# One decoder layer in split float32 on one core: where the low half of a sum is taken, where x is added, and how the first weights lie in memory

## The chip, the cores and the metric

The program runs on 1 core of one Trainium2 chip (trn2). The metric is device microseconds of one execution; the figure of a kernel is the median of its timed runs.

## The reference

A layer with two token mixers, 256 tokens of width 2048. Cut to what matters here:

```
h = rms_norm(x, norm_g)
proj = h @ w_in                                   # 2048 x 11264
q, k, v, z_a, u_b, v_b, z_b, g_a, g_b = split(proj)
att = moba_attention(rms_norm(q), rms_norm(k), v) # 8 heads, causal inside one block of 256
y_a = (att * silu(z_a)) @ w_proj_a
sgu = spatial_gating(gelu(u_b), gelu(v_b), sgu_norm_g, w_s, b_s)
y_b = (sgu * silu(z_b)) @ w_proj_b
merged = sigmoid(g_a) * y_a + sigmoid(g_b) * y_b
return x + merged @ w_out
```

All data are float32, and nearly all of the work is in the products with w_in, w_proj_a, w_proj_b and w_out.

## The kernel before, in words

**Splitting.** Each float32 operand is held as a high half (a cast to the type fp32r) and a low half (the value less its high half). A product is three matmuls of 128x512: low by high, high by high, high by low (`three`, line 415 and after; all of them have line 422 in the profile).

**Granules.** The weights come as 120 granules of 128x2048 float32 (1 MB), in the order of `schedule`. The blocks "quad" (q, k, v, za, vb, ub, zb, four g, two out, 8 granules each) multiply a 2x2 grid of blocks. A granule whose number is in the first tuple of its row in `SETS` is done by a Strassen-like form in seven products, 21 matmuls (`seven`); the others are done directly in eight, 24 matmuls (`direct`). The second tuple of the row is the order in which the granules of the block come. Between the g blocks stand the "proj" granules, 24 matmuls each. In the text below a granule of seven products is called S, one of eight D.

**The work on a granule ahead of its matmuls** is in `split`. For D: ACT casts the words to `wh` (line 244), DVE takes the low half in place (line 245). For S three sums of 512 columns are needed as well: `t[0]` (line 274), `t[1:3]` (line 275, which reads `t[0]`), their high half `th` by ACT (line 277), the low half of the words, 2048 columns in one instruction (line 279), and then the low half of the sums, 1536 columns (line 280). Before `t[0]` one block has to be added to another: in q, k and v DVE does that (line 272), in the later blocks a DMA adds in memory, from a copy of the block in a ring of 12 buffers (`pre_copy`, `pre_sum`), and the sum is loaded in place of the block.

**Order.** Every engine runs its list in the order in which the code emits it. Granule i's loop emits the loads of granule i+5 on SP, the matmuls of i on PE, and then the splits up to granule i plus its number in `LEADS`. All else (norms, softmax, transposes, evacuations) hangs on the loop by tables: `HOOKS` gives for each step its block, granule and place (pre, mid, late, evac, post), `EVAC` does so for the evacuation of PSUM and `SECOND` for the second half of a transposition. The words lie in six buffers (`words0` to `words5`, granule number modulo 6); a buffer takes its next load when PE is done with it. SP issues nearly all loads, strictly in order: an issue that has to wait holds back every later one.

**The start.** `LOADS` sets the order of the first loads: the first quarters of granule 0, the first columns of x, and so on. Granules 0 to 3 are loaded in pieces (`cuts`: four, four, two and two). While the first data come, 11 matmuls on zeros run (`ps_w`, line 322).

**The end.** The two out blocks (granules 104 to 111 and 112 to 119) each make four results of 128x512. `early` combines the S products of a block in SBUF tiles `e[0..3]`, and `residual` (lines 715 to 721) then adds x: in block 1 by DVE, from x in SBUF; in block 0 POOL issues four DMAs that add x to `e[j]` in SBUF (line 718), and SP stores each `e[j]` to the output (line 719). `post_out` later adds the D products of block 0 to the stored output, again by DMAs from POOL that add in memory (line 728).

Of the kernel before, what the change touches and what calls it, by code (L numbers as in the profile page):

```python
# [19 lines left out]
ALU = mybir.AluOpType  # L20
# [23 lines left out]
SETS = {("q", 0): ((), (0, 1, 2, 3, 4, 5, 6, 7)), ("k", 0): ((0, 1, 2, 3, 4), (5, 1, 3, 4, 6, 0, 2, 7)),  # L44
# [8 lines left out]
        ("out", 0): ((0, 1, 2, 4), (3, 2, 0, 6, 1, 7, 4, 5)),  # L53
        ("out", 1): ((0, 1, 2, 3, 4), (0, 5, 1, 2, 3, 4, 7, 6))}
SCRATCH = ("za", "vb", "ub", "zb", "g", "out")
LEADS = {("q", 0): (3, 2, 2, 3, 3, 3, 3, 2), ("k", 0): (2, 3, 3, 2, 3, 3, 3, 2),
# [16 lines left out]
SECOND = {("turn_m", 0): (1, "mid"), ("turn_m", 2): (1, "post"), ("turn_z", "za"): (1, "mid"),
          ("turn_qk", "q"): (1, "late"), ("mix", 0): (1, "mid"), ("turn_z", "zb"): (0, "post"),
          ("turn_qk", "k"): (1, "mid"), ("turn_m", 1): (1, "pre")}
HOOKS = [
    ("q", 0, 0, "pre", "split_x", 2), ("q", 0, 0, "pre", "split_x", 3), ("k", 0, 1, "evac", "root", "q", 2),
    ("q", 0, 1, "evac", "split_x", 5), ("q", 0, 2, "post", "split_x", 6), ("q", 0, 3, "mid", "split_x", 7),
    ("v", 0, 3, "late", "squares", "k", 3), ("q", 0, 4, "pre", "keep_vec"),
    ("ub", 0, 2, "pre", "squares", "vb", 0), ("ub", 0, 2, "evac", "squares", "vb", 1),  # L80
    ("q", 0, 5, "post", "forms", "x", "x"), ("vb", 0, 0, "mid", "func", "za", AF.Silu),
# [9 lines left out]
    ("v", 0, 3, "late", "norm", "k", 1), ("v", 0, 2, "late", "squares", "k", 2),
    ("k", 0, 4, "evac", "root", "q", 3), ("v", 0, 5, "late", "norm", "k", 2),
    ("v", 0, 0, "mid", "squares", "k", 0), ("q", 0, 1, "mid", "split_x", 4), ("zb", 0, 3, "late", "spatial"),
    ("proj", 3, 0, "evac", "func", ("g", 3), AF.Sigmoid), ("ub", 0, 3, "late", "root", "vb", 0),
# [50 lines left out]
def hybrid_layer_kernel(  # L145
# [54 lines left out]
    def f(ap):  # L200
        return ap.bitcast(F32)
# [729 lines left out]
```

## Time and profile before

| what | us |
|---|---|
| three timed runs | 661.92, 664.0, 933.4 |
| median | 664.0 |
| the profiled execution, its own time | 663.75 |
| its span, first to last instruction | 662.0 |
| PE busy / DVE busy / ACT busy in the span | 650.6 / 609.5 / 438.6 |

The span lies 1.75 us below the time of its own execution. A row of the timeline gives the start, the duration, the engine and line, the operation with what it writes and reads, the shape, and in brackets the idle time of the engine before it with what ended it. A row of the waits gives who waited for whom: the total, the number of times and the longest. In the names of the profile `words3float` is buffer 3 as it was loaded and `words3float32r` the same bytes as low halves. Matmuls overlap, so the cost of one is read from the distance of two starts and not from the duration.

### The profile page before, as it was taken

The page shows a single profiled execution, that of the slowest core. Times are in us where ns is not written, and L with a number is a line of the kernel's source. Part 1 is how long each engine was busy: PE and PEld are TensorE (multiplying, and loading weights), DVE is VectorE, ACT ScalarE, POOL GpSimd, SP SyncE. Part 2 cuts the span into 40 slices and gives each one's busy share as a digit, 9 for nine tenths or more (in the row PEclk, how much of TensorE's full clock was granted, in tenths as well). Part 3 has the DMA queues.
Part 4 walks back from the last instruction along what each step waited for, and adds up shares of the span by engine and source line. Part 5 has one row for each costly group of instructions (what it writes and reads, how often), then busy time and mean ns, then how long its engine had stood idle before and what let it go on. Part 6 is the DMA issues. An engine that isn't in the chain of part 4 may idle for free.

```text
span 662.0 us, 8169 instructions
## 1 busy us (share of the span) xinstructions
PE 650.6 (98%) x2956; PEld 535.5 (81%) x2956; DVE 609.5 (92%) x532; ACT 438.6 (66%) x547; POOL 89.7 (14%) x91
## 2 busy tenths in 40 slices
PE   9999999999999999999999999999999999999977
PEld 5888788888888888888887888888888888888855
DVE  4799999999999999999999999899978998999955
ACT  7969796968787598687556736655653567456540
POOL 1001323400010206210010011010101001100300
PEclk9999999999999999999999999999999999999979
DMA  8995587797777987986698579869966987974981
GB/s 298 417 364 204 203 253 254 228 260 220 230 211 247 271 258 235 282 255 238 189 324 252 171 228 338 266 218 313 288 227 209 328 264 233 259 237 169 165 278 63
DMA packets 46407, 164.71 MB, mean 249 GB/s; under 512 B 5152, under 2 KB 5792, under 8 KB 37792
## 3 DMA queue, kind: packets, MB, share of 16 engines
q1 hardware_dynamic: 36432, 146.11, 61.2%
q0 software_dynamic: 9360, 17.04, 16.6%
q10 hardware_dynamic: 576, 1.05, 0.4%
q8 instruction: 23, 0.38, 0.2%
q14 instruction: 16, 0.13, 0.1%
HBM read 159.46 MB, written 29.88 MB: 286 GB/s over the span
## 4 chain that ended last, share of the span: by engine, by line
PE 46%; DVE 36%; DMA 7%; issue 6%; ACT 3%; SPq 1%; POOL 0%; DVEq 0%; ACTq 0%; POOLq 0%
PE y L422 13%; PE acc_g L422 12%; PE seven_g L422 8%; PE acc_out L422 3%; PE acc_vb L422 2%; DVE sums0float32r L280 2%; PE acc_za L422 2%; DVE words2float32r L279 2%; DVE sums1float L275 2%; DVE sums2float32r L280 2%; PE seven_za L422 2%; DVE sums1float32r L280 2%; DVE sums0float L275 2%; DMA words5float<-in_w 2%; DMA cut_float<-in_w 2%
## 5 line engine op out<-in xcount | busy, mean ns | idle before, releaser
L229 POOL DMA_DIRECT2D ring<-in_w x51 | 43.4, 862 | 296.2 <-DMA ring<-in_w 288.6
L277 ACT CAST th<-sums1float 128x1536 fp32r<-128x1536 f32 x21 | 31.2, 1484 | 43.2 <-DVE sums1float L275 41.3
L277 ACT CAST th<-sums2float 128x1536 fp32r<-128x1536 f32 x20 | 29.7, 1486 | 45.1 <-DVE sums2float L275 45.1
L277 ACT CAST th<-sums0float 128x1536 fp32r<-128x1536 f32 x20 | 29.7, 1484 | 41.5 <-DVE sums0float L275 41.5
L367 POOL TENSOR_TENSOR rs<-ms,mhalf 128x4 f32<-128x4 f32 x12 | 30.4, 2533 | 74.9 <-DVE ms L366 74.9
L422 PE MATMUL acc_g<-wh,xuh 128*128 128x512 f32 x99 | 38.6, 389 | 0.0
L422 PE MATMUL acc_g<-wh,xul 128*128 128x512 f32 x99 | 38.6, 389 | 0.0
L280 DVE TENSOR_TENSOR sums1float32r<-sums1float,th 128x1536 fp32r<-128x1536 f32 x21 | 36.8, 1753 | 1.4 <-ACT th L277 1.4
L280 DVE TENSOR_TENSOR sums2float32r<-sums2float,th 128x1536 fp32r<-128x1536 f32 x20 | 35.1, 1753 | 0.0
L280 DVE TENSOR_TENSOR sums0float32r<-sums0float,th 128x1536 fp32r<-128x1536 f32 x20 | 35.1, 1753 | 0.0
L279 DVE TENSOR_TENSOR words2float32r<-words2float,wh 128x2048 fp32r<-128x2048 f32 x13 | 29.8, 2292 | 1.3
L245 DVE TENSOR_TENSOR words1float32r<-words1float,wh 128x2048 fp32r<-128x2048 f32 x10 | 22.9, 2288 | 7.1 <-ACT wh L244 7.1
L245 DVE TENSOR_TENSOR words5float32r<-words5float,wh 128x2048 fp32r<-128x2048 f32 x12 | 27.4, 2286 | 1.9 <-ACT wh L244 1.9
L422 PE MATMUL acc_out<-wh,ml 128*128 128x512 f32 x65 | 25.7, 396 | 2.2 <-ACT wh L267 2.2
L279 DVE TENSOR_TENSOR words4float32r<-words4float,wh 128x2048 fp32r<-128x2048 f32 x11 | 25.2, 2291 | 0.8
L422 PE MATMUL acc_out<-wh,mh 128*128 128x512 f32 x65 | 25.6, 393 | 0.0
L422 PE MATMUL y<-wh,zal 128*128 128x512 f32 x64 | 25.2, 394 | 0.0
L422 PE MATMUL acc_q<-wh,xuh 128*128 128x512 f32 x64 | 25.2, 393 | 0.0
L422 PE MATMUL y<-wh,zbl 128*128 128x512 f32 x64 | 25.0, 391 | 0.0
L422 PE MATMUL acc_q<-wh,xul 128*128 128x512 f32 x64 | 25.0, 391 | 0.0
L422 PE MATMUL y<-wh,zah 128*128 128x512 f32 x64 | 25.0, 390 | 0.0
L422 PE MATMUL y<-wh,zbh 128*128 128x512 f32 x64 | 24.9, 390 | 0.0
(992 smaller groups left out, 2172.8 us busy)
## 6 DMA issues: line engine op xcount, KB each, us to landing
words5float<-in_w SPq DMA_DIRECT2D x14, 1024.0 KB, 7.8
ring<-in_w SPq DMA_DIRECT2D x51, 256.0 KB, 7.4
ring<-in_w POOLq DMA_DIRECT2D x51, 256.0 KB, 7.2
words1float<-in_w SPq DMA_DIRECT2D x12, 1024.0 KB, 6.5
words4float<-in_w SPq DMA_DIRECT2D x11, 1024.0 KB, 8.9
words3float<-in_w SPq DMA_DIRECT2D x11, 1024.0 KB, 7.0
words0float<-in_w SPq DMA_DIRECT2D x9, 1024.0 KB, 7.1
words2float<-in_w SPq DMA_DIRECT2D x11, 768.0 KB, 6.9
```

The source lines that it names most:

```text
L229: nc.gpsimd.dma_start(pre[i], w[i, :, 2 * B:3 * B], accum_op=ALU.add)
L245: nc.vector.tensor_tensor(l, r, f(h), op=ALU.subtract)
L275: nc.vector.tensor_tensor(*(ap.rearrange("p (a n) -> p a n", n=B) for ap in (t[:, B:], r[:, 2 * B:])), t[:, None, 0:B].to_broadcast([P, 2, ...
L277: nc.scalar.copy(th[i], t)
L279: nc.vector.tensor_tensor(wl[i], r, f(wh[i]), op=ALU.subtract)
L280: nc.vector.tensor_tensor(tl[i], t, f(th[i]), op=ALU.subtract)
L367: nc.gpsimd.tensor_tensor(dst, ms[:, :n], mhalf[:, :n], op=ALU.pow)
L422: nc.tensor.matmul(acc, a, b, start=(start and n == 0), stop=(stop and n == 2))
```

## The change

**1. Sums.** The low half of the sums of an S granule (before: line 280, right behind the words' low half) is kept back and emitted by `settle`: between the two sums of the next granule if that is S, ahead of its split if it is D.

**2. Half tiles.** The words of an S granule are two tiles of 128x1024, loaded by separate DMAs, cast by two ACT instructions and turned to low halves by two DVE instructions.

**3. x.** In out block 0 SP stores `e[j]` first, and POOL's DMA then adds x to the stored output in memory. `post_out` adds the rest as before.

**4. Layout.** The host lays each piece of granules 0 to 3 (`CUTS`) in one run of memory; the piece had been rows of 2 or 4 KB at steps of 8 KB.

**5. Tables.** k does four granules by sevens in place of five (7 x 3 = 21 matmuls become 24 for one granule). The other blocks keep their number of S granules; orders, leads, hooks and evacuation places are new. The matmuls on zeros are 8 in place of 11, and one pair of the `four_forms` subtractions is swapped.

The diff, with the tables cut to `SETS` and the hooks at the start of the program:

```diff
-SETS = {("q", 0): ((), (0, 1, 2, 3, 4, 5, 6, 7)), ("k", 0): ((0, 1, 2, 3, 4), (5, 1, 3, 4, 6, 0, 2, 7)),
+SETS = {("q", 0): ((), (0, 1, 2, 3, 4, 5, 6, 7)), ("k", 0): ((0, 1, 2, 3), (5, 3, 4, 1, 6, 0, 2, 7)),
...
-        ("out", 0): ((0, 1, 2, 4), (3, 2, 0, 6, 1, 7, 4, 5)),
-        ("out", 1): ((0, 1, 2, 3, 4), (0, 5, 1, 2, 3, 4, 7, 6))}
+        ("out", 0): ((0, 1, 2, 4), (3, 0, 5, 6, 1, 2, 4, 7)),
+        ("out", 1): ((0, 1, 2, 3, 4), (5, 2, 3, 0, 4, 1, 6, 7))}
...
-    ("q", 0, 0, "pre", "split_x", 2), ("q", 0, 0, "pre", "split_x", 3), ("k", 0, 1, "evac", "root", "q", 2),
-    ("q", 0, 1, "evac", "split_x", 5), ("q", 0, 2, "post", "split_x", 6), ("q", 0, 3, "mid", "split_x", 7),
...
+    ("q", 0, 0, "post", "split_x", 5), ("q", 0, 2, "late", "split_x", 7), ("v", 0, 3, "mid", "squares", "k", 3),
...
+CUTS = {0: 4, 1: 4, 2: 2, 3: 2}
...
+    HW = WORDS // 2
+    halfs = [[both(f"half{n}_{j}_", HW, base + 8 * KB * n + j * 4 * KB) for j in range(2)] for n in range(RAWS)]
...
     def load_piece(i, a, b):
-        nc.sync.dma_start(raw[i][:, a:b], w[i, :, a:b])
+        src = w[i, :, a:b]
+        if i in CUTS:
+            n = WORDS // CUTS[i]
+            j = a // n
+            src = bass.AP(tensor=w.tensor, offset=w.offset + (i * WORDS + j * n) * P + a - j * n,
+                          ap=[[n, P], [1, b - a]])
+        nc.sync.dma_start(raw[i][:, a:b], src)
...
             nc.sync.dma_start(raw[i][:, 0:B], pre[i])
-            load_piece(i, B, WORDS)
+            load_piece(i, B, HW)
+            load_piece(i, HW, WORDS)
             return
+        if strassen(i):
+            pieces = 2
...
         if i in pre:
-            nc.scalar.copy(wh[i], r)
+            nc.scalar.copy(wh[i][:, 0:HW], h0)
+            nc.scalar.copy(wh[i][:, HW:], h1)
             mid()
...
-        nc.vector.tensor_tensor(t[:, 0:B], r[:, 0:B], r[:, B:2 * B], op=ALU.subtract)
-        nc.vector.tensor_tensor(*(ap.rearrange("p (a n) -> p a n", n=B) for ap in (t[:, B:], r[:, 2 * B:])),
+        nc.vector.tensor_tensor(t[:, 0:B], h0[:, 0:B], h0[:, B:HW], op=ALU.subtract)
+        settle()
+        nc.vector.tensor_tensor(*(ap.rearrange("p (a n) -> p a n", n=B) for ap in (t[:, B:], h1)),
                                 t[:, None, 0:B].to_broadcast([P, 2, B]), op=ALU.subtract)
         nc.scalar.copy(th[i], t)
         late()
-        nc.vector.tensor_tensor(wl[i], r, f(wh[i]), op=ALU.subtract)
-        nc.vector.tensor_tensor(tl[i], t, f(th[i]), op=ALU.subtract)
+        nc.vector.tensor_tensor(l0, h0, f(wh[i][:, 0:HW]), op=ALU.subtract)
+        nc.vector.tensor_tensor(l1, h1, f(wh[i][:, HW:]), op=ALU.subtract)
+        unsettled.append((i, t))
+
+    unsettled = []
+
+    def settle(i=NG):
+        if unsettled and unsettled[0][0] <= i:
+            n, t = unsettled.pop()
+            nc.vector.tensor_tensor(tl[n], t, f(th[n]), op=ALU.subtract)
...
-    for _ in range(11):
+    for _ in range(8):
         nc.tensor.matmul(ps_w, warm[:, 0:P], warm, start=True, stop=True)
...
             if c == 0:
-                nc.gpsimd.dma_start(e[j], part(x, c, j), accum_op=ALU.add)
                 nc.sync.dma_start(part(out, c, j), e[j])
+                nc.gpsimd.dma_start(part(out, c, j), part(x, c, j), accum_op=ALU.add)
...
         plain = i < 8
+        settle(i)
...
+    for i, n in CUTS.items():
+        g[i] = g[i].reshape(P, n, WORDS // n).transpose(1, 0, 2).reshape(P, WORDS)
```

**SP at the end, before.** The issues from the last load of granule 116 (`words2`) to the loads of granule 117 (`words3`) and 118; in brackets what each waits for (DMASW are DMAs that POOL issued, DMAHW those of the other queues).

```order
L217 DMA words2float_59<-in_w 128x1536 [waits DMAHW7_49]
L719 DMA out<-out_c_4605 128x512 [waits DMAHW0_49,DMASW1_49]
L719 DMA out<-out_c_4608 128x512 [waits DMAHW1_49,DMASW2_49]
L719 DMA out<-out_c_4607 128x512 [waits DMAHW2_49,DMASW3_49]
L719 DMA out<-out_h 128x512 [waits DMAHW3_49,DMASW4_49]
L236 DMA words3float_61<-ring_121 128x512 [waits DMASW0_49,DMAHW4_49,DVE_49,PE_49]
L217 DMA words3float_61<-in_w 128x1536 [waits DMAHW5_49]
L217 DMA words4float_63<-in_w 128x2048 [waits DMAHW6_49,DVE_49,PE_49]
```

The same place in the changed kernel (`half_0_79` and `half_1_81` are buffer 3).

```order
L226 DMA half_1_float_77<-in_w 128x1024 [waits DMAHW2_49]
L746 DMA out<-out_c_4792 128x512 [waits DMAHW3_49,Activation_49]
L746 DMA out<-out_c_4795 128x512 [waits DMAHW4_49,DVE_49]
L746 DMA out<-out_c_4794 128x512 [waits DMAHW5_49,DVE_49]
L746 DMA out<-out_h 128x512 [waits DMAHW6_49,DVE_49]
L247 DMA half_0_float_79<-ring_145 128x512 [waits DMAHW7_49,DMASW0_49,PE_49]
L226 DMA half_0_float_79<-in_w 128x512 [waits DMAHW0_49]
L226 DMA half_1_float_81<-in_w 128x1024 [waits DMAHW1_49]
L226 DMA words4float_63<-in_w 128x2048 [waits DMAHW2_49,PE_49]
```

The four stores stand at the same place, ahead of granule 117's loads; they wait for the engines that make `e[j]` and no longer for POOL's DMAs.

**DVE in a run of S granules, before** (three granules in out block 1; `sums` are the sums of a granule, `th` their high half).

```order
L274 TENSOR_TENSOR sums1float_93<-words0float_55 128x512
L275 TENSOR_TENSOR sums1float_93<-words0float_55,sums1float_93 128x1024
L279 TENSOR_TENSOR words0float32r<-words0float_55,wh_4664 128x2048
L280 TENSOR_TENSOR sums1float32r<-sums1float_93,th_4665 128x1536
L274 TENSOR_TENSOR sums2float_95<-words1float_57 128x512
L275 TENSOR_TENSOR sums2float_95<-words1float_57,sums2float_95 128x1024
L279 TENSOR_TENSOR words1float32r<-words1float_57,wh_4698 128x2048
L280 TENSOR_TENSOR sums2float32r<-sums2float_95,th_4699 128x1536
```

The same engine in a run of S granules of out block 1 in the changed kernel.

```order
L293 TENSOR_TENSOR sums0float_115<-half_0_float_67 128x512
L308 TENSOR_TENSOR sums2float32r<-sums2float_119,th_4757 128x1536
L295 TENSOR_TENSOR sums0float_115<-half_1_float_69,sums0float_115 128x1024
L299 TENSOR_TENSOR half_0_float32r<-half_0_float_67,wh_4852 128x1024
L300 TENSOR_TENSOR half_1_float32r<-half_1_float_69,wh_4852 128x1024
L293 TENSOR_TENSOR sums1float_117<-half_0_float_71 128x512
L308 TENSOR_TENSOR sums0float32r<-sums0float_115,th_4853 128x1536
L295 TENSOR_TENSOR sums1float_117<-half_1_float_73,sums1float_117 128x1024
L299 TENSOR_TENSOR half_0_float32r<-half_0_float_71,wh_4862 128x1024
L300 TENSOR_TENSOR half_1_float32r<-half_1_float_73,wh_4862 128x1024
```

The instruction of line 280 (now 308) has moved from the end of its own granule to between the two sums of the next, and the words' low half is two instructions of half the width.

More of the change, by code (lines that the diff above doesn't have):

```diff
@@ L73 @@
[L73 to L74 removed]
+SETS = {("q", 0): ((), (0, 1, 2, 3, 4, 5, 6, 7)), ("k", 0): ((0, 1, 2, 3), (5, 3, 4, 1, 6, 0, 2, 7)),
[8 rows of a table added]
+        ("out", 0): ((0, 1, 2, 4), (3, 0, 5, 6, 1, 2, 4, 7)),
+        ("out", 1): ((0, 1, 2, 3, 4), (5, 2, 3, 0, 4, 1, 6, 7))}
+SCRATCH = ("za", "vb", "ub", "zb", "g", "out")
+LEADS = {("q", 0): (3, 2, 2, 2, 2, 3, 3, 2), ("k", 0): (2, 3, 3, 2, 2, 2, 2, 2),
[5 rows of a table added]
+         ("out", 1): (3, 2, 3, 3, 3, 3, 3, 2), ("proj", 0): (3, 2, 3, 3), ("proj", 1): (2, 2, 3, 3),
+         ("proj", 2): (2, 2, 3, 2), ("proj", 3): (3, 3, 3, 2)}
@@ new lines @@
+EVAC = {("proj", 0): (0, "late"), ("proj", 1): (0, "evac"), ("proj", 2): (1, "mid"), ("proj", 3): (0, "late"),
+        ("g", 2, "quad"): (0, "late"), ("zb", 0, "early"): (1, "late"), ("out", 1, "quad"): (0, "evac"),
+        ("g", 3, "quad"): (0, "mid"), ("k", 0, "early"): (0, "evac"), ("vb", 0, "quad"): (1, "pre"),
+        ("v", 0, "quad"): (0, "mid"), ("g", 0, "early"): (0, "late"), ("g", 1, "early"): (0, "evac"),
+        ("v", 0, "early"): (0, "pre"), ("out", 1, "early"): (1, "late"), ("out", 0, "quad"): (0, "evac"),
+        ("za", 0, "early"): (0, "pre"), ("g", 3, "early"): (0, "evac"), ("q", 0, "quad"): (0, "mid"),
+        ("out", 0, "early"): (1, "mid"), ("zb", 0, "quad"): (1, "pre"), ("ub", 0, "early"): (0, "evac"),
+        ("vb", 0, "early"): (0, "evac"), ("za", 0, "quad"): (0, "evac"), ("ub", 0, "quad"): (1, "late"),
+        ("g", 2, "early"): (1, "pre"), ("q", 0, "early"): (1, "late"), ("k", 0, "quad"): (0, "evac"),
+        ("g", 0, "quad"): (0, "mid")}
@@ L91 @@
[L91 to L94, printed above, removed]
-    ("g", 0, 0, "mid", "func", "zb", AF.Silu), ("ub", 0, 3, "evac", "squares", "vb", 2),
-    ("ub", 0, 6, "evac", "norm", "vb", 1), ("v", 0, 4, "late", "root", "k", 2),
@@ new lines @@
+    ("q", 0, 2, "evac", "split_x", 6), ("za", 0, 2, "late", "soft_max", 0), ("zb", 0, 0, "post", "mix", "E"),
[5 rows of a table added]
+    ("ub", 0, 5, "evac", "norm", "vb", 1), ("proj", 3, 0, "mid", "turn_m", 2, (0, 1), "L01"),
+    ("zb", 0, 3, "evac", "spatial"), ("ub", 0, 3, "late", "squares", "vb", 3), ("q", 0, 3, "mid", "load_nat"),
[3 rows of a table added]
+    ("proj", 2, 0, "late", "func", ("g", 2), AF.Sigmoid), ("za", 0, 1, "post", "score", "E"),
+    ("ub", 0, 7, "pre", "norm", "vb", 3), ("za", 0, 4, "mid", "soft_exp", 1),
+    ("proj", 0, 1, "post", "func", ("g", 0), AF.Sigmoid), ("vb", 0, 0, "late", "turn_p", 0, "E012"),
@@ new lines @@
+    ("ub", 0, 4, "evac", "norm", "vb", 0), ("q", 0, 6, "pre", "stats"), ("za", 0, 3, "late", "soft_max", 1),
+    ("v", 0, 5, "post", "norm", "k", 3), ("ub", 0, 6, "evac", "norm", "vb", 2), ("q", 0, 2, "mid", "split_x", 4),
+    ("proj", 3, 2, "mid", "halves_h", "m"), ("vb", 0, 2, "post", "attend", 1, "E23"),
+    ("v", 0, 0, "post", "root", "k", 0), ("q", 0, 0, "pre", "split_x", 2), ("za", 0, 5, "post", "soft_sum", 1),
+    ("ub", 0, 3, "evac", "root", "vb", 0), ("proj", 3, 1, "post", "forms", "mf", "m"),
@@ new lines @@
+    ("k", 0, 4, "late", "norm", "q", 0), ("k", 0, 1, "mid", "squares", "q", 1),
+    ("v", 0, 4, "late", "root", "k", 2), ("ub", 0, 1, "post", "func", "vb", AF.Gelu_apprx_tanh),
+    ("k", 0, 7, "late", "norm", "q", 3), ("proj", 3, 2, "post", "halves_l", "m"),
+    ("proj", 3, 2, "post", "turn_m", 1, (0, 1), "L23"), ("ub", 0, 2, "late", "squares", "vb", 1),
+    ("out", 0, 0, "in", "turn_m", 3, (0, 1), "E01"), ("out", 0, 2, "late", "forms_m4"),
+    ("out", 0, 3, "mid", "halves_m4"), ("g", 0, 5, "post", "gate_b"), ("vb", 0, 1, "in", "turn_p", 1, "E301"),
@@ L117 @@
+    ("proj", 1, 0, "mid", "func", ("g", 1), AF.Sigmoid), ("vb", 0, 2, "late", "load_mix"),
+    ("proj", 3, 1, "post", "func", ("g", 3), AF.Sigmoid), ("q", 0, 5, "late", "forms_5"),
     ("out", 1, 2, "post", "load_res", 1),
```

65 lines of the change are left out of this document (21 added, 44 removed), and 40 rows, old and new, of tables (HOOKS, LEADS, SETS).

## The prediction, made before the changed kernel ran

> **What bounds the kernel now.** First the page, for who is busy; then the chain of waits, for the rate at which PE runs when nothing holds it; then what PE waited for; then the timeline at those places.
>
> ```profile
> span 662.0 us, 8169 instructions
> PE 650.6 (98%) x2956; PEld 535.5 (81%) x2956; DVE 609.5 (92%) x532; ACT 438.6 (66%) x547; POOL 89.7 (14%) x91
> ```
>
> ```profile
> 422.22 21.79 PE y L422 x96
> ```
>
> PE is busy for 98% of the span, DVE for 92%. In the chain 96 matmuls of 128x512 take 21.79 us, 0.227 us each; that is PE's own pace, and only time beyond it can be won without taking matmuls away. DVE is second in line and close. Where PE stood still:
>
> ```profile
> PE acc_out L422 <- ACT wh L267: 2.2, 1, 2.2
> PE acc_out L422 <- DVE words3float32r L279: 1.4, 1, 1.4
> ...
> PE acc_g L422 <- DVE words2float32r L279: 0.9, 1, 0.9
> PE acc_k L422 <- DVE words2float32r L279: 0.5, 1, 0.5
> ```
>
> Two waits at the end of the program and two on DVE at granules with sums are all that reach half a microsecond once the layer's matmuls have begun; each costs more than its row says.
>
> **The stall at the end.**
>
> ```profile
> 635.07 0.39 PE L422 MATMUL acc_out<-sums0float32r,mh 128*128 128x512 f32 x1
> 637.68 0.69 PE L422 MATMUL acc_out<-wh,ml 128*128 128x512 f32 x1 [2.22 <-ACT wh L267]
> ...
> 641.17 0.63 PE L422 MATMUL acc_out<-wh,F5h 128*128 128x512 f32 x1
> 641.60 0.63 PE L422 MATMUL acc_out<-words3float32r,F5h 128*128 128x512 f32 x1
> ...
> 644.84 0.39 PE L422 MATMUL seven_out<-th,F5h 128*128 128x512 f32 x1
> ```
>
> and, as a row of the stages (busy time of PE, PEld, DVE, ACT and POOL, then granted clock, DMA share and GB/s):
>
> ```profile
> 634.80:645.00 10.20, 6.63 (x17) 4.45 (x17) 8.17 (x5) 7.13 (x5) 0.00 (x0) 0.67 0.70 259
> ```
>
> From 635.07 to 644.84 lie 14 starts. At 0.227 they take 3.2 us; they took 9.8. The stall costs 6.6 us, of which the two waits are 3.6. The rest is the pace afterwards: starts 0.43 us apart, with a granted clock of 0.67 in that window.
>
> Why it stood:
>
> ```profile
> 611.02 0.59 ACT L727 COPY late<-acc_out 128x512 f32<-128x512 f32 x1 [0.77 <-PE acc_out L422]
> 615.05 0.88 POOL L718 DMA_DIRECT2D out_h<-in_x  x1 [0.29 <-issue]
> 614.76 6.21 SPq L719 DMA_DIRECT2D out<-out_c  x3
> 622.92 0.33 SPq L719 DMA_DIRECT2D out<-out_h  x1
> 623.42 1.91 SPq L236 DMA_DIRECT2D words3float<-ring  x1
> 635.75 0.69 DVE L274 TENSOR_TENSOR sums1float<-words3float 128x512 f32<-128x512 f32 x1 [5.62 <-DMA words3float<-in_w]
> ```
>
> PE was done with the last granule of out block 0 by 611.02, so buffer 3 was free. But SP stood in front of its four stores, each of which waited for POOL's addition of x to land, until 622.92. Only then did it issue granule 117's load (623.42), which took until 635.7: 12.3 us.
>
> **The change, part by part.**
>
> *x in memory.* The stores now wait for DVE's and ACT's four tiles alone. In the rows, POOL's last addition, which needed the last of these tiles, was issued at 615.05, so all tiles were there by then. Four stores at the 0.33 us of the single issue are 1.3 us: granule 117's load goes out at about 616.4 (615.05 + 1.3) instead of 623.42. With the same 12.3 us it lands at 628.7. DVE had its previous sums done at 635.75 - 5.62 = 630.1. So the load is 1.4 us early and the stall goes: **-6.6**. What is late next: the additions to the output. They are as many as before:
>
> ```profile
> out<-out_c SPq DMA_DIRECT2D x6, 256.0 KB, 2.7
> out<-late POOLq DMA_DIRECT2D x4, 256.0 KB, 9.0
> ```
>
> Store, addition of x, addition of the rest: 2.7 + 9.0 + 9.0 us plus eight issues on POOL of 0.88 (7 us) from 616 end near 644, ahead of the end at about 653. On POOL nothing but these additions is queued there. Cost 0; without that cover it is the last rival below.
>
> *Sums and half tiles.* One granule on DVE, start to start:
>
> ```profile
> 332.96 0.69 DVE L274 TENSOR_TENSOR sums2float<-words0float 128x512 f32<-128x512 f32 x1
> 333.68 1.23 DVE L275 TENSOR_TENSOR sums2float<-words0float,sums2float 128x1024 f32<-128x1024 f32 x1
> 335.00 2.29 DVE L279 TENSOR_TENSOR words0float32r<-words0float,wh 128x2048 fp32r<-128x2048 f32 x1
> 337.21 1.75 DVE L280 TENSOR_TENSOR sums2float32r<-sums2float,th 128x1536 fp32r<-128x1536 f32 x1
> 338.88 0.68 DVE L274 TENSOR_TENSOR sums0float<-words1float 128x512 f32<-128x512 f32 x1
> 137.08 1.88 DVE L484 TENSOR_TENSOR v_c<-acc_v,v_c 128x512 f32<-128x512 f32 x3
> 16.84 4.63 DVE L245 TENSOR_TENSOR cut_float32r<-cut_float,wh 128x1024 fp32r<-128x1024 f32 x4 [0.26 <-ACT wh L244]
> ```
>
> The period is 5.92: 0.72 + 1.32 + 2.21 + 1.67. Three instructions of 512 columns that do not wait for each other take 1.88, 0.60 from start to start; four of 1024 take 4.63, 1.14 each. So the second sum, which reads the first, costs 0.12 extra, and what follows it 0.18. With the late low half between the two sums the first gap goes; if the half tile frees the second gap as well, the period is 0.60 + 1.67 + 3 x 1.14 = 5.69, a gain of 0.23. If it does not, 5.87, a gain of 0.05; if each half pays the gap instead, 6.05 to 6.2, a loss of up to 0.3. I take 0.1 to 0.2: the independent rows are the nearer ones, since the first half touches nothing that the second sum reads or writes. Over the 34 such granules up to the first g block (5 + 5 + 5 + 4 + 4 + 6 + 5) that is 3 to 7 us of DVE. In k there is more:
>
> ```profile
> 77.20 0.68 DVE L272 TENSOR_TENSOR words2float<-words2float 128x512 f32<-128x512 f32 x1
> 83.93 2.28 DVE L245 TENSOR_TENSOR words3float32r<-words3float,wh 128x2048 fp32r<-128x2048 f32 x1
> ```
>
> A granule by sevens costs 6.73 there, a direct one 2.2: 4.5 us of DVE less, for three matmuls more, 3 x 0.227: **+0.7**. ACT does two casts for one; it idles for a third of the span.
>
> What PE gets of this is only its stalls. The largest:
>
> ```profile
> 347.93 0.39 PE L422 MATMUL acc_g<-wh,xuh 128*128 128x512 f32 x1
> 349.20 0.50 PE L422 MATMUL acc_g<-words2float32r,xuh 128*128 128x512 f32 x1 [0.89 <-DVE words2float32r L279]
> ```
>
> 1.27 between starts, 1.04 lost, for a wait shown as 0.9. The two rows of waits on DVE sum to 1.4; scaled alike, with smaller ones and some after-effect, 2 to 2.8. DVE's relief exceeds each of them, so I take **-2.3** (bounds 0, if the new tables put other work in front, and -2.8).
>
> *Layout, warm matmuls and the first hooks.*
>
> ```profile
> 1.25 4.88 PE L322 MATMUL ps_w<-warm 128*128 128x512 bf16 x11 [1.25 <-DVE warm L319]
> 5.47 0.62 ACT L244 CAST wh<-cut_float 128x512 fp32r<-128x512 f32 x1 [1.44 <-DMA cut_float<-in_w]
> 7.20 0.39 PE L422 MATMUL acc_q<-wh,xuh 128*128 128x512 f32 x1
> 13.13 0.40 PE L422 MATMUL acc_q<-wh,xuh 128*128 128x512 f32 x1
> 13.74 0.50 PE L422 MATMUL acc_q<-cut_float32r,xuh 128*128 128x512 f32 x1 [0.21 <-DVE cut_float32r L245]
> ```
>
> The first matmul needs ACT's first cast, which waits for a landing until 5.47 and ends at 6.09; it does not follow the warm run. Pieces in one run can only land earlier or alike; nothing in the trace prices it: 0 to -1, and I take **-0.5**, about the loss before 13.74 (0.61 less 0.227) and a little of the first landing. The warm run shrinks to 8/11 of 4.88, 3.5 us, and ends near 4.8, over 1 us before the data. I take 0 for that and price it below.
>
> Sum on the span: 662.0 - 6.6 + 0.7 - 2.3 - 0.5 = 653.3. Around the span lie 663.75 - 662.0 = 1.75 us: **655.1**. The median of the runs, 664.0, is within 0.3 of the profiled one.
>
> **The rivals.**
>
> *A cold start.* After the stall at the end, starts were 0.43 apart from 637.68 to 644.6, 7 us, though PE had work. If the gap after the shorter warm run does the same, 7 us from 6.1 on hold 16 matmuls that each lose 0.2: 3.2, less the 0.5 booked above. 657.8. For it: before, PE came to full pace at about 7.2, right after an unbroken run from 1.25. Against it: the gap would be some 1.3 us, half of the 2.6 between the starts at 635.07 and 637.68.
>
> [...]
>
> *The stall stays.* The load's margin is 1.4 us, and it now shares the DMA engines with the additions in memory. A landing 4 us later brings the stall and the slow pace back: 655.1 + 6.6 = 661.7. For it: the 12.3 us of the late load. Against it: DVE may be further ahead, and PE needs granule 117 only at 635.
>
> *DVE gains nothing for PE*, or the new orders bring as many stalls: 655.1 + 2.3 + about 1 = 658.4. For it: the low half of the sums did not wait for ACT before either.
>
> *Slower: the additions become the end.* All eight write one output. If each waits for the one before to land, 8 x 9.0 = 72 us from 616 end at 688, some 690 us. It decides once the chain passes about 652, that is 36 us or four landings. Against it: before, the four additions of line 728 were issued apart by less than a landing.
>
> **How the numbers follow.** The forecast 0.58; cold start 0.18; DVE gains nothing 0.12; the stall stays 0.08; slower 0.04. The range goes from 652.5, all stalls gone and a start 1 us earlier, to 661.0, over the second and third cases. Two per cent, about what a measurement of this kernel can tell from no change, is 13.3 us: faster would need 650.7, below the sum of all bounds, 0.03; slower needs 677.3, the last case, 0.04; within, 0.93.
>
> **What would show it.** Right: no PE gap over 0.5 us after 600, and SP's stores of block 0 within 2 us; DVE's period near 5.7 in a run of granules with sums; no wait of PE on a low half of words before 350. Wrong: starts 0.43 apart beyond 9 us; a DMA of line 756 landing after PE's last matmul; a span above 658.

## The result, and the profile after

| | before | changed |
|---|---|---|
| median of the runs, us | 662.97 (4 runs) | 657.90 (657.48 to 658.04, 4 runs) |
| profiled execution, us | 663.75 | 658.03 |
| its span, us | 662.0 | 655.2 |

The ratio of the times is 0.9929, with a 95% interval of 0.991 to 0.9948: about 5 us less, within the two per cent that were called no change. One run of before, at 933.4 us, is left out of the ratio as disturbed; the other three took 661.92, 661.94 and 664.0. The forecast was 655.1, the range 652.5 to 661.0.

The head of the page of the changed kernel:

```profile
span 655.2 us, 8445 instructions
PE 646.4 (99%) x2956; PEld 534.0 (81%) x2956; DVE 602.4 (92%) x588; ACT 442.0 (67%) x605; POOL 86.8 (13%) x91
```

PE is now busy for 99% of its span. What it still waited for:

```profile
PE ps_m L646 <- DVE ub_c L512: 2.1, 1, 2.1
PE ps_w L350 <- DVE warm L347: 1.3, 1, 1.3
PE acc_g L450 <- DVE half_float32r L300: 0.6, 1, 0.6
```

Both waits at the end are gone, the wait in the first g block is there still (0.6 for 0.9, at 349.29), and one is new: the matmuls of the spatial mixing (`ps_m`) wait 2.1 us for DVE's evacuation of `ub_c`.

Where the 6.8 us of the span lie is read from the start of each block's first matmul:

| stretch | before, us | changed, us | difference |
|---|---|---|---|
| span's start to k | 50.89 | 50.40 | -0.49 |
| k to zb (k, v, za, vb, ub) | 223.37 | 221.82 | -1.55 |
| zb | 43.48 | 45.82 | +2.34 |
| g, y and proj | 251.18 | 251.14 | -0.04 |
| out, to its last matmul's start | 88.42 | 81.59 | -6.83 |
| after that | 4.66 | 4.43 | -0.23 |

The end, first. SP and POOL in the changed kernel (issues; line 746 stores block 0, 747 adds x to it, 247 and 226 load granule 117, 756 adds the rest):

```profile
609.09 2.60 SPq L746 DMA_DIRECT2D out<-out_c  x3
612.09 0.33 SPq L746 DMA_DIRECT2D out<-out_h  x1
612.52 0.39 SPq L247 DMA_DIRECT2D half_float<-ring  x1
612.97 0.93 SPq L226 DMA_DIRECT2D half_float<-in_w  x2
```

```profile
612.22 0.82 POOL L747 DMA_DIRECT2D out<-in_x  x1 [33.83 <-DMA out<-out_c]
...
621.29 0.84 POOL L747 DMA_DIRECT2D out<-in_x  x1 [4.57 <-DMA out<-in_x]
626.12 0.90 POOL L756 DMA_DIRECT2D out<-late  x1 [3.99 <-DMA out<-in_x]
...
634.01 0.85 POOL L756 DMA_DIRECT2D out<-late  x1 [0.41 <-issue]
```

Granule 117's load goes out at 612.5 instead of 623.4, and DVE doesn't wait for it (it shows no idle time from 605 to 647.12). The waiting has moved to POOL, where an addition waits for one before it (4.57, 3.99). The last is issued at 634.0; the additions of line 756 took 4.9 to 11.0 us to land, so it is done by 645, ahead of PE's last matmul at 650.8.

Then the new wait. Before, PE went into the mixing without one, and DVE's evacuation of `ub` (line 484) came behind two sums:

```profile
279.47 0.39 PE L422 MATMUL acc_zb<-words0float32r,xuh 128*128 128x512 f32 x1
279.70 2.84 PE L618 MATMUL ps_m<-vb_c,ws 128*128 128x128 f32 x24
```

```profile
275.35 0.68 DVE L274 TENSOR_TENSOR sums1float<-words2float 128x512 f32<-128x512 f32 x1
276.06 1.23 DVE L275 TENSOR_TENSOR sums1float<-words2float,sums1float 128x1024 f32<-128x1024 f32 x1
277.20 1.88 DVE L484 TENSOR_TENSOR ub_c<-acc_ub,ub_c 128x512 f32<-128x512 f32 x3
```

PE and DVE in the changed kernel (line 512 evacuates `ub`, 308 is the kept-back low half of sums, 548 multiplies `vb` by its gain):

```profile
277.43 0.39 PE L450 MATMUL acc_zb<-words0float32r,xuh 128*128 128x512 f32 x1
279.97 2.92 PE L646 MATMUL ps_m<-vb_c,ws 128*128 128x128 f32 x24 [2.15 <-DVE ub_c L512]
```

```profile
263.00 0.69 DVE L548 TENSOR_TENSOR vb_c<-vb_c,gain 128x512 f32<-128x512 f32 x1 [2.16 <-ACT vb_c L545]
264.80 2.29 DVE L259 TENSOR_TENSOR words0float32r<-words0float,wh 128x2048 fp32r<-128x2048 f32 x1 [1.11 <-ACT wh L258]
...
275.73 0.69 DVE L293 TENSOR_TENSOR sums0float<-half_float 128x512 f32<-128x512 f32 x1
276.33 1.75 DVE L308 TENSOR_TENSOR sums2float32r<-sums2float,th 128x1536 fp32r<-128x1536 f32 x1
278.00 1.22 DVE L295 TENSOR_TENSOR sums0float<-half_float,sums0float 128x1024 f32<-128x1024 f32 x1
279.14 1.88 DVE L512 TENSOR_TENSOR ub_c<-acc_ub,ub_c 128x512 f32<-128x512 f32 x3
```

PE came to the mixing 2 us earlier than before, and DVE to the evacuation 1.94 us later (279.14 for 277.20). Most of the 1.94 is the kept-back low half: from the first sum to the evacuation DVE takes 3.41 for 1.85, 1.56 more. The other 0.38 it is late already at the first sum (275.73 for 275.35); it has idled 2.16 and 1.11 for ACT at the norms of `vb`, which the new hooks order anew.

### The profile page after: what moved, and what is told of

It reads as the page before. It is cut to its first block, busy times and chain, and to the rows that moved or that the text cites. A ratio compares the mean times of both kernels' runs of the same rounds, so it can differ in the third digit from the quotient of the medians.

```text
span 655.2 us, 8445 instructions
## 1 busy us (share of the span) xinstructions
PE 646.4 (99%) x2956; PEld 534.0 (81%) x2956; DVE 602.4 (92%) x588; ACT 442.0 (67%) x605; POOL 86.8 (13%) x91
## 3 DMA queue, kind: packets, MB, share of 16 engines
q10 hardware_dynamic: 576, 1.05, 0.8%
## 4 chain that ended last, share of the span: by engine, by line
PE 85%; DVE 7%; DMA 2%; issue 2%; POOL 2%; ACT 1%; SPq 0%; DVEq 0%; ACTq 0%
PE acc_g L450 14%; PE y L450 13%; PE acc_out L450 9%; PE seven_g L450 9%; PE acc_q L450 6%; PE acc_vb L450 5%; PE acc_k L450 5%; PE acc_v L450 4%; PE seven_out L450 4%; PE acc_zb L450 3%; PE seven_zb L450 3%; PE seven_v L450 2%; PE acc_za L450 2%; PE seven_vb L450 2%; PE seven_k L450 2%
## 5 line engine op out<-in xcount | busy, mean ns | idle before, releaser
L299 DVE TENSOR_TENSOR half_float32r<-half_float,wh 128x1024 fp32r<-128x1024 f32 x60 | 73.2, 1219 | 0.2
L300 DVE TENSOR_TENSOR half_float32r<-half_float,wh 128x1024 fp32r<-128x1024 f32 x60 | 73.1, 1219 | 0.0
L297 ACT CAST th<-sums1float 128x1536 fp32r<-128x1536 f32 x20 | 29.7, 1485 | 41.3 <-DVE sums1float L295 41.3
L284 ACT CAST wh<-half_float 128x1024 fp32r<-128x1024 f32 x51 | 53.4, 1048 | 6.0 <-issue 3.6
L285 ACT CAST wh<-half_float 128x1024 fp32r<-128x1024 f32 x51 | 53.5, 1049 | 0.0
L395 POOL TENSOR_TENSOR rs<-ms,mhalf 128x4 f32<-128x4 f32 x12 | 27.8, 2343 | 72.6 <-DVE ms L394 72.6
L308 DVE TENSOR_TENSOR sums1float32r<-sums1float,th 128x1536 fp32r<-128x1536 f32 x20 | 35.0, 1752 | 0.0
L259 DVE TENSOR_TENSOR words4float32r<-words4float,wh 128x2048 fp32r<-128x2048 f32 x12 | 27.4, 2287 | 1.9 <-ACT wh L258 1.8
L259 DVE TENSOR_TENSOR words5float32r<-words5float,wh 128x2048 fp32r<-128x2048 f32 x11 | 25.1, 2285 | 1.7 <-ACT wh L258 1.7
L259 DVE TENSOR_TENSOR words1float32r<-words1float,wh 128x2048 fp32r<-128x2048 f32 x9 | 20.6, 2286 | 5.3 <-ACT wh L258 5.3
```

The lines of the kernel that those rows point to most:

```text
L259: nc.vector.tensor_tensor(l, r, f(h), op=ALU.subtract)
L284: nc.scalar.copy(wh[i][:, 0:HW], h0)
L285: nc.scalar.copy(wh[i][:, HW:], h1)
L297: nc.scalar.copy(th[i], t)
L299: nc.vector.tensor_tensor(l0, h0, f(wh[i][:, 0:HW]), op=ALU.subtract)
L300: nc.vector.tensor_tensor(l1, h1, f(wh[i][:, HW:]), op=ALU.subtract)
```

## The experiments

Each was timed beside the kernel before on the same chip; the ratios are to that. "Changed" is the changed kernel.

**x alone.** The kernel before with only the order of store and addition turned round.

```diff
-                nc.gpsimd.dma_start(e[j], part(x, c, j), accum_op=ALU.add)
                 nc.sync.dma_start(part(out, c, j), e[j])
+                nc.gpsimd.dma_start(part(out, c, j), part(x, c, j), accum_op=ALU.add)
```

> The kernel before, with nothing changed but the order of the store and the addition of x in out block 0. Theory (the whole gain is the stall at the end, caused by SP standing behind POOL's additions): no PE gap over 0.5 us after 600, PE's last matmul 6.6 us earlier than 657.3, span about 655.4, time about 656.4 against 663.0 (ratio 0.990), so as fast as the whole change or faster. Rival (the stall at the end went because the new orders of the out blocks put the loads or the sums earlier): the gap at 635 stays at 2 us or more and the time stays above 660.

657.91 us (657.45 to 659.1), ratio 0.9936 (0.992 to 0.9953). After 351.2 us PE loses nothing; the out blocks take 81.78 us to the start of their last matmul for 88.42, 6.64 less, as the theory had it. The last matmul starts at 652.71, not at 650.7, and the time is 1.5 us above the expected: the profiled execution lost 1.3 us more than that of before ahead of k, and 1.7 more in zb. By the medians (657.91 and 657.90) this one swap gives the whole gain of the change, and everything else in it adds up to nothing.

**The layout alone.** The kernel before with the `CUTS` part of the diff.

```diff
-        nc.sync.dma_start(raw[i][:, a:b], w[i, :, a:b])
...
+            src = bass.AP(tensor=w.tensor, offset=w.offset + (i * WORDS + j * n) * P + a - j * n,
+                          ap=[[n, P], [1, b - a]])
+        nc.sync.dma_start(raw[i][:, a:b], src)
```

> The kernel before, with nothing changed but the layout of granules 0 to 3 in runs (11 warm matmuls as before). Theory (the pieces land earlier, and PE then waits for the next ones): ACT's first cast starts near 4.1 in place of 5.5; the first matmul is held by the warm run until about 6.0, so PE's first start moves by 0.1 to 0.2 only, the waits between 12 and 14 shrink by up to 0.6, and by the k block PE is 0.2 to 0.6 us ahead; time 662.4 to 662.8 against 663.0. Rival (the early start of the changed kernel comes from its first hooks): first cast at 5.5 as before, nothing ahead at k.

661.95 us (661.25 to 663.18, 10 runs), ratio 0.9992 (0.9982 to 1.0003). ACT's first cast starts at 4.39 for 5.47 and the first matmul at 5.57 for 6.14, but k at 51.34 for 50.89 and not earlier: PE has the first words earlier and stands for the later ones (0.57 us in three waits from 12 to 14.3, for one of 0.21). By itself no gain that can be measured; with the old layout, too, the start of k varies from one profile to the next (50.89 in that of before, 52.20 in the run with x alone).

**The evacuation earlier.** The changed kernel with the evacuation of `ub` ahead of the next granule's sums.

```diff
-("ub", 0, "quad"): (1, "late")
+("ub", 0, "quad"): (1, "mid")
```

> The changed kernel, with one entry of the evacuation table changed: the ub block's results are added ahead of the next granule's sums and not behind them, so that the deferred low half of 1.67 us and two sums no longer stand in front of them. Theory (the 2.1 us wait of the mix matmuls on DVE at 277 is a loss of its own, made by what stands in front of the evacuation): the wait goes, the g block starts 2 us earlier, and the time falls by 1.5 to 2.3 us, to about 656. Rival (DVE is the bound from zb to the first g block, so the time lost at 277 is paid later): the wait at 277 goes, but the wait near 348 grows from 0.6 to 2 us or more, and the time stays within 0.5 us of 657.9.

660.83 us (659.26 to 662.07, 10 runs), ratio 0.997 (0.9953 to 0.9986): 3 us slower than the changed kernel, which neither side had expected. The wait at 277 went, and the next one was worse. ACT, and then PE, in that run:

```profile
280.60 1.48 ACT L297 CAST th<-sums0float 128x1536 fp32r<-128x1536 f32 x1 [5.79 <-DVE sums0float L295]
...
283.87 3.20 ACT L655 ACTIVATE vb_c<-ps_m,vec 128x128 f32<-128x128 f32 x12
```

```profile
281.32 0.39 PE L450 MATMUL acc_zb<-half_float32r,Fhx 128*128 128x512 f32 x1
285.05 0.50 PE L450 MATMUL seven_zb<-wh,xul 128*128 128x512 f32 x1 [3.35 <-ACT vb_c L655]
...
287.12 0.80 PE L450 MATMUL seven_zb<-wh,Flx 128*128 128x512 f32 x1 [1.11 <-ACT vb_c L655]
287.72 0.63 PE L450 MATMUL seven_zb<-wh,Fhx 128*128 128x512 f32 x1
```

The evacuation pushed the sums back on DVE. ACT's cast `th` waits for the second sum, and behind `th` in ACT's list stand the readings of `ps_m` (283.87 for 282.53), whose PSUM PE needs. After a second wait, of 1.11, PE ran at 0.43 from start to start up to 292. So the place of the evacuation alone was not the fault: whichever DVE does first, evacuation or sums, PE waits for what hangs on the other.

**No deferral.** The changed kernel with the low half of the sums at its old place, at the end of its own granule.

```diff
-        unsettled.append((i, t))
+        nc.vector.tensor_tensor(tl[i], t, f(th[i]), op=ALU.subtract)
```

> The changed kernel, with the low half of the sums taken right behind its granule's words as before the change (half tiles kept). Theory (the deferral takes 0.12 us per granule out of DVE's gaps, but pushes the ub evacuation back by 1.67 us): DVE's period in a run of sums becomes 5.80 in place of 5.68, the wait at 277 shrinks by 1.5 us or more, other waits on DVE before 350 grow by 1 to 2 us in all; time 657.0 to 658.5, no clear difference. Rival 1 (the deferral is worth its place): slower by 2 us or more. Rival 2 (the deferral only costs): faster by 1.5 us or more, no new wait.

656.09 us (655.09 to 656.93), ratio 0.9905 (0.9889 to 0.9922). The wait at the mixing is gone, and the first g block starts at 315.72 for 318.04. DVE's period is 5.80 for 5.68, as expected. By the medians it is 1.8 us faster than the changed kernel, the size that the second rival had (the two intervals overlap a little), but not without a new loss: at 443.10 (1.23, and 0.40 at 445.12) PE waits for the products of a proj granule to be merged (line 713), at 443.82, which now stand behind the low half at 442.15. In the next run, with deferral on this stretch, they are merged at 440.87, and PE does not wait.

**Deferral from granule 56 on**, that is, from the first g block.

```diff
+        if i < 56:
+            nc.vector.tensor_tensor(tl[i], t, f(th[i]), op=ALU.subtract)
+        else:
             unsettled.append((i, t))
```

> The changed kernel, with the low half of the sums deferred only from the first g block on (granule 56); before that it is taken at once. Theory (the deferral has two effects on PE: it holds up the ub evacuation and the mix matmuls at 277, a loss of 2.3 us, and it lets the proj results be added sooner near 443, a gain of 1.6 us): both waits are absent, the g block starts near 315.7 and the second g block near 442, PE's last matmul comes near 649.0, time 655.0 to 655.8, 1 us below the version with no deferral at all. Rival (DVE is the bound and gives back later what it gains): some wait on DVE of 1 us or more appears after 350 and the time is that of no deferral, 656.1.

654.45 us (653.8 to 654.66), ratio 0.9881 (0.9867 to 0.9896), clear of the changed kernel's interval and 0.5 us below the theory's range. What PE still lost from k on is one wait, 0.72 us at 345.14:

```profile
PE acc_g L453 <- DVE half_float32r L300: 0.6, 1, 0.6
```

The last matmul starts 3.2 us earlier than in the changed kernel, 2.8 of it in zb.

**x back in the tiles.** The changed kernel with POOL's addition ahead of the store, as before.

```diff
+                nc.gpsimd.dma_start(e[j], part(x, c, j), accum_op=ALU.add)
                 nc.sync.dma_start(part(out, c, j), e[j])
-                nc.gpsimd.dma_start(part(out, c, j), part(x, c, j), accum_op=ALU.add)
```

> The changed kernel with the old order of x in out block 0 (POOL adds x to the tiles in SBUF, then SP stores): all of the change but that. Theory (x is the gain, and SP behind POOL is its mechanism): SP's stores spread over 7 us or more again, granule 117's load goes out near 621, PE waits 2 us or more near 633 and then runs at 0.43 between starts; 6 to 7 us slower than the changed kernel, 663.5 to 665, no faster than the kernel before. Rival (the new order of the out blocks hides a late load, since granule 117 now follows a longer run of sums): 658 to 660.

660.89 us (658.45 to 662.52, 10 runs), ratio 0.997 (0.9952 to 0.9988): 3.0 us slower than the changed kernel, between the theory's range and the rival's. SP, PE, ACT and DVE in that run:

```profile
614.26 5.33 SPq L747 DMA_DIRECT2D out<-out_c  x3
621.66 0.33 SPq L747 DMA_DIRECT2D out<-out_h  x1
622.16 0.33 SPq L247 DMA_DIRECT2D half_float<-ring  x1
```

```profile
637.07 0.50 PE L450 MATMUL acc_out<-half_float32r,mh 128*128 128x512 f32 x1 [1.32 <-DVE half_float32r L300]
```

```profile
642.72 1.91 ACT L258 CAST wh<-words5float 128x2048 fp32r<-128x2048 f32 x1 [2.83 <-DMA words5float<-in_w]
```

```profile
644.66 2.29 DVE L259 TENSOR_TENSOR words5float32r<-words5float,wh 128x2048 fp32r<-128x2048 f32 x1 [2.44 <-ACT wh L258]
646.87 0.68 DVE L505 TENSOR_TENSOR out_h<-seven_out,out_c 128x512 f32<-128x512 f32 x1
```

The jam on SP is the same as before, but it shows in two places: PE loses 1.5 us at 635 and keeps its pace of 0.227 afterwards, and DVE comes to the last combinations at 646.87 instead of 640.91, so that the program's end lies 6.8 us behind the start of PE's last matmul, not 4.4. So here the late load was not paid on PE alone.

**11 matmuls on zeros.** The changed kernel with the old number.

```diff
-    for _ in range(8):
+    for _ in range(11):
```

> The changed kernel with 11 warm matmuls in place of 8. Theory (with the early landing the longer warm run only holds PE; what PE gains by starting earlier it loses again in waits for the next pieces by 13 us): first matmul of the layer near 5.6 in place of 4.7, waits up to 14 us smaller by about 0.7, the k block within 0.4 us of the 50.4 of the changed kernel, time 657.7 to 658.3. Rival (the shorter run costs pace): faster than the changed kernel by 1 us or more.

657.70 us (657.43 to 657.97), ratio 0.9932 (0.9917 to 0.9947): no difference.

**The old rows with 8 matmuls on zeros.** The changed kernel without the layout.

```diff
-        if i in CUTS:
-            n = WORDS // CUTS[i]
...
-    for i, n in CUTS.items():
-        g[i] = g[i].reshape(P, n, WORDS // n).transpose(1, 0, 2).reshape(P, WORDS)
```

> The changed kernel with the first granules in rows as before (so that the first data land as late as before) and still 8 warm matmuls: it makes the idle second after the warm run that the prediction feared. Cold-start theory: the granted clock falls or does not rise, starts 0.43 us apart from 6.1 on for 3 to 7 us, the k block at 52 or later, time 659 to 661. Rival (a gap of 1.3 us costs no pace): starts 0.43 apart end by about 7.5, the k block at 50.5 to 51.3, time 658.0 to 658.8.

658.76 us (658.41 to 659.5), ratio 0.995 (0.9935 to 0.9964), 0.9 us above the changed kernel by the medians, with intervals that overlap. In its pace this is the cold start of the prediction's first rival, in its time it is not (659 to 661 was expected of it). PE in this run:

```profile
1.26 3.59 PE L345 MATMUL ps_w<-warm 128*128 128x512 bf16 x8 [1.26 <-DVE warm L342]
6.06 0.80 PE L445 MATMUL acc_q<-wh,xuh 128*128 128x512 f32 x1 [1.21 <-ACT wh L253]
6.65 0.63 PE L445 MATMUL acc_q<-wh,xul 128*128 128x512 f32 x1
...
9.21 0.63 PE L445 MATMUL acc_q<-wh,xul 128*128 128x512 f32 x1
9.64 0.46 PE L445 MATMUL acc_q<-cut_float32r,xuh 128*128 128x512 f32 x1
```

After an idle time of 1.21 the starts are 0.43 apart from 6.65 to 9.21, and the pace is full from 9.64 on, 3.6 us after the first matmul. The granted clock doesn't show it, as a row of the stages (its third number from the end) says:

```profile
6.06:9.64 3.58, 3.58 (x8) 2.77 (x9) 2.96 (x5) 3.15 (x7) 0.00 (x0) 1.00 1.05 362
```

The slow pace costs less than it looks: eight starts 0.2 late are 1.6 us, but the waits for words at 11 to 13 us, in which the changed kernel loses 1.2, are not there, and k starts 1.05 us later.

**The old tables.** The changed kernel's code with all tables of before (`SETS`, `LEADS`, `EVAC`, `SECOND`, `HOOKS`), of which a line:

```diff
-("k", 0): ((0, 1, 2, 3), (5, 3, 4, 1, 6, 0, 2, 7))
+("k", 0): ((0, 1, 2, 3, 4), (5, 1, 3, 4, 6, 0, 2, 7))
```

> The changed kernel with all five tables of the kernel before (which granules are done by sevens, orders, leads, evacuation places, hooks), so it keeps x in memory, layout, 8 warm matmuls, half tiles and the deferral. Theory (x in memory brings nearly all of the gain; tables and the rest cancel out): 656.5 to 658.5. If the new tables matter for it: 660 or more, with waits of PE on DVE over 1 us in k or at the mix. If the new tables cost: below 656.

656.15 us (655.61 to 656.95), ratio 0.9909 (0.9893 to 0.9926), just under the theory's range: by the medians the new tables cost 1.8 us here, though the intervals overlap. No wait at the mixing; losses of 0.84 at 64.95, 0.51 at 306.6 and 1.03 at 578.6, each on the second half of a granule's words.

**The old tables without deferral.** The kernel of the run above, with the edit of the run without deferral:

```diff
-        unsettled.append((i, t))
+        nc.vector.tensor_tensor(tl[i], t, f(th[i]), op=ALU.subtract)
```

> The kernel of the old tables (x in memory, layout, 8 warm matmuls, half tiles) without the deferral. Theory (the deferral is worth 0.12 us per granule wherever DVE is what PE waits for, and costs only where something urgent stands behind it, which these tables do not have at the mix): waits near 65, 307 and 579 longer by 0.3 to 1 us each, 0.5 to 1.5 us slower than 656.15. Rival (the deferral costs under these tables too): faster than 655.7.

654.03 us (653.19 to 655.03), ratio 0.9872 (0.9853 to 0.9892). Deferral costs 2.1 us under the old tables too, by intervals that just part; the rival held. DVE with the old tables and deferral, at the first of the three losses:

```profile
60.12 0.69 DVE L293 TENSOR_TENSOR sums0float<-half_float 128x512 f32<-128x512 f32 x1
60.73 1.75 DVE L308 TENSOR_TENSOR sums2float32r<-sums2float,th 128x1536 fp32r<-128x1536 f32 x1
62.40 1.22 DVE L295 TENSOR_TENSOR sums0float<-half_float,sums0float 128x1024 f32<-128x1024 f32 x1
...
64.74 1.22 DVE L300 TENSOR_TENSOR half_float32r<-half_float,wh 128x1024 fp32r<-128x1024 f32 x1
```

and without it:

```profile
60.68 0.69 DVE L293 TENSOR_TENSOR sums0float<-half_float 128x512 f32<-128x512 f32 x1
61.41 1.23 DVE L295 TENSOR_TENSOR sums0float<-half_float,sums0float 128x1024 f32<-128x1024 f32 x1
...
63.76 1.22 DVE L300 TENSOR_TENSOR half_float32r<-half_float,wh 128x1024 fp32r<-128x1024 f32 x1
```

From the first sum to line 300 it takes 4.62 with deferral and 3.08 without, 1.54 more: the 1.67 of the moved instruction less the 0.12 gap that it fills. PE wants the words at 64.95; without deferral it loses nothing there.

**Whole tiles.** The kernel before with x in memory, the layout, 8 matmuls on zeros and the swapped pair of forms, without half tiles and new tables (loads and ACT's casts are whole again too). Against the run above, on DVE:

```diff
-        nc.vector.tensor_tensor(l0, h0, f(wh[i][:, 0:HW]), op=ALU.subtract)
-        nc.vector.tensor_tensor(l1, h1, f(wh[i][:, HW:]), op=ALU.subtract)
+        nc.vector.tensor_tensor(wl[i], r, f(wh[i]), op=ALU.subtract)
```

> The kernel before with x added in memory, the first granules in runs, 8 warm matmuls and the new order of the forms, but with whole tiles of words and the tables of before: against the run with the old tables, half tiles and no deferral (654.03) only the half tiles are missing. Theory (the words of a granule in two halves let DVE's second half and PE's use of the first run apart, and this takes away DVE's stalls in zb and in the first g, 1.6 + 1.0 us in the run that only adds x in memory, down to 0.7 + 0.4): 656.0 to 657.4, PE waits of 0.4 us and over on a low half of words near 303, 308 and 348. Rival (the half tiles give PE nothing, and 654.0 comes from the start and from x): 653.6 to 654.8, and the waits near 303 to 348 as small as with half tiles.

656.54 us (656.0 to 658.12), ratio 0.9908 (0.9878 to 0.9937), as the theory had it: PE loses 0.57 at 80.70, 1.03 at 306.77 and 1.05 at 348.10 on a low half of words. With half tiles (the run above) these are 0.34, 0.67 and 0.42, in all 1.2 us less. By the two medians half tiles are worth 2.5 us; the intervals of the two ratios overlap, so the size is uncertain, and the waits are the firmer sign.

**The old tables, deferral from granule 56 on.** The run with the old tables and half tiles, with the same edit as under the new tables:

```diff
+        if i < 56:
+            nc.vector.tensor_tensor(tl[i], t, f(th[i]), op=ALU.subtract)
+        else:
+            unsettled.append((i, t))
```

> The run of 654.03 (tables of before, half tiles) with the sums' low half between the next two sums, from granule 56 on only. Theory (each deferral puts 1.67 us of DVE between the two sums, and where DVE enters a run late, PE waits for the low half of words behind it): the wait of 1.0 us at 578 and that of 0.5 us at 306, which the deferral showed under these tables, come back if the granules there are number 56 or later, the waits in k do not: 654.8 to 655.6. Rival (the deferral shortens DVE's period by 0.12 and only the early granules pay for it, as under the new tables, where deferral from granule 56 on gained 1.6 us over none): 652.2 to 653.4.

654.75 us (654.4 to 655.16), ratio 0.9879 (0.9849 to 0.9908): just under the theory's range and clear of the rival's. PE again loses 1.03, at 577.31. DVE there:

```profile
571.50 1.35 DVE L672 TENSOR_TENSOR ml<-ps_mT,mh 128x512 fp32r<-128x512 f32 x2 [3.24 <-ACT mh L671]
572.76 0.68 DVE L293 TENSOR_TENSOR sums0float<-half_float 128x512 f32<-128x512 f32 x1
573.36 1.75 DVE L311 TENSOR_TENSOR sums2float32r<-sums2float,th 128x1536 fp32r<-128x1536 f32 x1
```

DVE has just idled 3.24 us for ACT, enters the granule late, and does another granule's low half first. The 0.51 at 306 doesn't come back (0.14 is left); zb's granules come before 56. But that loss does not hang on deferral alone, since the run without deferral lost 0.67 there. In the first g block PE no longer waits for a low half of words, where the run without deferral lost 0.42; whether the shorter period does this is not shown.

All together, with half tiles, x in memory and the layout in each (us, and the ratio to before):

| | no deferral | from granule 56 | everywhere |
|---|---|---|---|
| tables of before | 654.03 (0.9872) | 654.75 (0.9879) | 656.15 (0.9909) |
| new tables | 656.09 (0.9905) | 654.45 (0.9881) | 657.90 (0.9929), the change |

The three lowest can't be told apart by their intervals. With deferral from granule 56 on, the tables make no difference.

## Why the prediction was right and where it failed

The time lies in the range, 2.8 us above the forecast, and within two per cent of before, as forecast. By its steps:

- **The end, -6.6.** Right for the profiled execution: -6.83, and the jam on SP was the cause. But the profiled execution of before had a long stall. With the same out blocks, the run with the layout alone took 90.98 us from its first out matmul to its end for 93.08, and PE waited there once, for 1.57; by the medians the swap was worth 5.2 us when made alone and 3.0 when taken back. That SP's stores would all go within 2 us was not so: they go as their tiles come, over 3.3 us from 609.1. It costs nothing.
- **Three more matmuls in k, +0.7.** They are in the -1.55 of the stretch from k to zb, which without them would be -2.2.
- **DVE's relief, -2.3: the step that failed.** The prediction said that DVE's relief exceeds each of PE's stalls, and so takes them away. DVE's period did fall as worked out, to 5.68 (forecast 5.69), as the changed kernel's rows show:

```profile
283.80 0.69 DVE L293 TENSOR_TENSOR sums1float<-half_float 128x512 f32<-128x512 f32 x1
284.40 1.75 DVE L308 TENSOR_TENSOR sums0float32r<-sums0float,th 128x1536 fp32r<-128x1536 f32 x1
...
289.48 0.69 DVE L293 TENSOR_TENSOR sums2float<-half_float 128x512 f32<-128x512 f32 x1
```

  But a period says when DVE is done with many granules, and PE's stalls ask when it is done with one. Counted from its first sum, the moved instruction made a granule's words 1.54 us later, which PE felt where DVE came late into a run; and at the mixing it pushed an evacuation behind PE (a wait of 2.15). The wait on a low half of words at 349, which was to go, lost 0.78 still, for 1.04. From k to out the stretches changed by -2.2 + 2.34 - 0.04, about 0.1, in place of -2.3. How much of the -2.2 is relief of DVE and how much is work that the new tables moved was not separated. This is what the third rival said, at 658.4, with a chance of 0.12. It had the event and not the cause: it feared that the low half had no wait to lose, while the cause was what it was put in front of.
- **Tables.** Neither tables nor deferral make the wait at the mixing alone. The evacuation of `ub` starts at 279.14 in the changed kernel, for which PE is ready at 277.66. Without the deferral it starts at 276.21 and PE comes at 278.13; with the tables of before it starts at 277.43 and PE comes at 279.00. In both the wait is gone. Which of the tables' entries does it was not separated.
- **The start, -0.5.** The size was right, the way was not: the first words land earlier (ACT's first cast at 4.07 for 5.47, and at 5.39 in the run with the old rows; the median from issue to landing is 5.0 us for 5.4 in the pieces of 256 KB and 6.9 for 7.1 in those of 512 KB), the first matmul starts 1.4 us earlier (4.74 for 6.14), and 0.9 of it is given back by k, in waits for later words. That pieces in one run could only land earlier or alike was the author's assumption; these medians agree with it and show no more. That the size agrees is in part luck: in the profiles of the runs that keep this layout and 8 matmuls on zeros, k starts anywhere from 49.34 to 50.63.
- **The cold start, 657.8.** It did not happen (from 5.80 on the changed kernel's starts are about 0.23 apart), and the agreement with the measured time is chance. What that rival feared did show with 8 matmuls on zeros and the old rows, where starts were 0.43 apart from 6.65 to 9.21 after an idle time of 1.21. It cost about 0.9, not 3.2: the slow pace ended at 9.64 and not after 7 us, and the changed kernel, without it, lost 1.2 in waits for data at 11 to 13 us. With the layout the first matmul comes at 4.74, right behind the matmuls on zeros, and 8 or 11 of them make no difference (657.90 and 657.70).
- **The additions at the end.** They do wait for each other in part (4.57 and 3.99 us on POOL), which was the last rival's mechanism; they end some 6 us before PE's last matmul and cost nothing.
- **Around the span, 1.75.** In the profiled execution it was 2.83, in the four runs 1.74 to 2.83, in those of other kernels up to 2.96; what makes it is open. With the span 1.9 above the forecast it makes up the miss. The start of the sum was high as well: 663.75 and the median of 664.0 stood at the upper end, since two of the other three runs of before took 661.9.

What a wait does to PE's pace differs from place to place. PE kept its 0.227 over the wait of 2.15 at the mixing, and over those of 1.57 and 1.32 at the end in the runs with the layout alone and with x back in the tiles. It lost it at the end of before, where waits of 2.22 and 1.35 follow each other within 5.1 us. In the run with the earlier evacuation it had it for three matmuls after a wait of 3.35 and lost it after a second one, of 1.11. At the start of the run with the old rows and 8 matmuls on zeros, starts were 0.43 apart after a single idle time of 1.21. The length of a wait alone does not order these cases, and no run shows what else decides.

## What to carry to other kernels

A queue that issues loads should not hold stores that wait for a slow engine (here this cost 3 to 5 us): let the store go first, and add in memory. Moving an instruction into another chain's gap can shorten the period and lengthen that chain (here 5.68 for 5.80, and 4.62 for 3.08 under the old tables); look at the places where the engine arrives late, after an evacuation or a wait, and leave the move out there. Parts of a change that each look like relief are best timed apart: here x in memory, the layout, 8 matmuls on zeros and half tiles with the old tables gave 654.0, and the rest, deferral and new tables, gave 3.9 us back.

## What was not expected of the hardware

- Two waits of PE of nearly one length, 2.15 and 2.22 us, left its pace as it was in one place and halved it in another (0.43 from start to start for 0.227, up to 7 us after it), where a second wait, of 1.35, followed.
- At the start of the run with the old rows and 8 matmuls on zeros, the starts were 0.43 apart for 3 us while the records gave a clock of 1.00.
- Half pace at the start cost about 0.9 us in the time, where eight matmuls lost 0.2 each: at full pace the changed kernel waited 1.2 us for words later.
- Two dependent sums on DVE left a gap of 0.12, which the independent low half between them filled: 0.60 + 1.67 from the first sum to the second with one between, 0.72 without.
